# The border between the first feed-forward and the mixers of a hybrid decoder layer, written out as one order, with two mixer weights split ahead of it

## The chip, the cores and the metric

The kernel runs on one core of a Trainium2 chip. The metric is the device time of one launch in microseconds (us). The kernel before took 933.62 us (median of 3 runs, 933.32 to 933.72). One more execution was taken with the hardware profiler: it took 932.9 us, of which its instructions span 930.8 us, so 2.1 us lie around the span. All times of day below (such as "at 338.34") are us from the start of that span.

## What is computed

One decoder layer on 512 tokens of width 1024, in float32:

```python
x = x + 0.5 * rms_norm(swiglu_ffn(rms_norm(x, norm_pre[l, 0]), ffn1_w_in[l], ffn1_w_out[l]), norm_post[l, 0])
mixed = token_mixer(rms_norm(x, norm_pre[l, 1]), w_mix_in[l], ..., w_mix_out[l])
x = x + rms_norm(mixed, norm_post[l, 1])
x = x + 0.5 * rms_norm(swiglu_ffn(rms_norm(x, norm_pre[l, 2]), ffn2_w_in[l], ffn2_w_out[l]), norm_post[l, 2])
```

`swiglu_ffn` has an inner width of 2816. `token_mixer` multiplies the normed tokens by one wide matrix `w_mix_in`, runs two recurrences (HGRN2 and mLSTM) on the columns in chunks, gates and norms them, and multiplies by `w_mix_out`. The first 512 columns that the kernel takes from `w_mix_in` are the forget gates of HGRN2: a sigmoid, then `log`, then a running sum.

## The kernel before: how the work is laid out

**Tiles.** The 512 tokens lie in four tiles of 128 (tile 0 to 3). `xs` holds the residual x in float32. `xq` (four buffers, `xq_77` to `xq_80` in the order of instructions) holds the normed tokens transposed, split into a high and a low part; `xq0` and `xq1` hold tiles 0 and 1, `xq2` and `xq3` tiles 2 and 3.

**Products.** A float32 product is done as three TensorE products (PE): high by high, high by low, low by high. So each weight tile of 512 KB is loaded by DMA into a `raw` buffer (issued on the queue of SP), and then split: ScalarE (ACT) casts it to the high part (`cast`, L235), VectorE (DVE) subtracts to get the low part (L236). A split weight goes into one of `WBUF` = 4 slots of one large tile `w`. `split` (L189) does the next weight of a fixed list; `feed` splits while fewer than 4 slots are taken; `pull` calls `feed` and hands out the next split weight; `drop` frees a slot. Splitting a weight is also what issues a later load: the `raw` ring of the mixers' weights has three buffers, so load n+3 goes out once weight n is split.

**The end of the first feed-forward** (`ffn_out`, L699). The output is made in two halves of 512 columns. In the second half the first seven pairs of weight rows are done in one loop; the last four pairs (`LAST`) are left to the end, and then done tile by tile, so that the tiles become ready one after the other. The six matmuls of one tile with one of these pairs are called a half-pair here (`out_mm`, L721, matmuls at L130 to L132). Some pairs are done in a seven-product form whose corrections (`terms`) are added to the sums by DVE (`add`, L756). For tile 3 that is done ahead: one matmul (L796) opens another PSUM bank, `add` writes sum plus correction into it, and the last pairs go on there. For tiles 0 to 2 `add` comes after the last matmul. In the order of before, `mm(0)` does the last four pairs for tiles 0 and 1 in turn, and then come tiles 2 and 3.

**From a finished tile to the mixers** (`last`, L429, outside any written schedule: a scheduler orders the instructions of each engine). `post1` squares the second half of the tile on ACT (L377), makes the norm's factor with two tiny POOL (GpSimd) instructions (L378, L382), multiplies by the gain (DVE, L414) and adds to `xs` (two DVE instructions, L418). `pre` norms the new x for the mixers: two ACT squares of `xs`, three POOL instructions, two DVE products (L396) into `xn` (tiles 0 and 2, one buffer) or into a free part of `hf` (tiles 1 and 3). `turn` transposes it on PE (8 matmuls by the identity, L291), and `two` splits the result from PSUM: ACT copies the high part (L297), DVE the low part (L298).

**The head of the mixers.** `head4` (L472) multiplies the first four mixer weights (the forget gates, w0 to w3 below) by tiles 0 and 1 alone (`head_mm`, 24 matmuls each, L467), before tiles 2 and 3 are ready, and turns tiles 2 and 3 after the first and third of them. Then `forget_gates` (L1023) multiplies the same four weights by tiles 2 and 3 (L457), takes the sigmoids and so on; from there on, jobs of further mixer weights (`job_f`, `job_t`) are dealt out between the steps of the recurrences. All of that is ordered by the scheduler.

Of the kernel before, what the change touches and what calls it, by code (L numbers as in the profile page):

```python
# [14 lines left out]
P = 128  # L15
T = 512
D = 1024
# [6 lines left out]
PAIRS = NF // 2  # L24
HALF = T // 2
# [45 lines left out]
class Layer:  # L71
# [201 lines left out]
    def drop(self, w):  # L273
        self.alive -= 1
        self.free.append(self.slot.pop(id(w))[0])
# [109 lines left out]
    def pre(self, i, g):  # L385

        nc = self.nc
        x = self.xs[:, i, :]
        *_, r = self.rms([x[:, :512], x[:, 512:]])
        if i % 2:  # L390
            xn = self.hf[:, 16:18, :].rearrange("p a t -> p (a t)")
        else:
            xn = self.sp.tile([P, D], F32, tag="xn", bufs=1, name=self.name("xn"))
        for h in range(2):
            v = slice(512 * h, 512 * h + 512)
            scaled = nc.vector.scalar_tensor_tensor(xn[:, v], x[:, v], r, g[:, v], op0=ALU.mult, op1=ALU.mult)  # L396
        self.normed = [self.square, scaled]
        return xn
# [54 lines left out]
    def in_k(self, ps, w, k, hs):  # L453
        mm = self.nc.tensor.matmul
        for n, (a, b) in enumerate(((0, 0), (0, 1), (1, 0))):
            for m, (u0, u1) in enumerate(hs):
                mm(  # L457
                    ps[:, u0:u1], w[:, a, k, :], self.xop(k, b, u0, u1),
                    start=k + n + m == 0, stop=k == ND - 1 and n == 2, skip_group_check=True,
                )  # L460

    def head_mm(self, w):

        ps = self.ps()
        for m, (a, b) in enumerate(((0, 0), (1, 0), (0, 1))):
            for k in range(ND):
                self.nc.tensor.matmul(  # L467
                    ps[:, :HALF], w[:, a, k, :], self.xop(k, b, 0, HALF), start=m + k == 0, stop=m == 2 and k == ND - 1
                )
        self.head.append((w, ps))  # L470

    def head4(self, trans):  # L472

        self.head = []
        for n in range(4):
            self.head_mm(self.pull())
            if n in (0, 2):
                trans(2 + n // 2)

    def open_ffn(self, ctx):  # L480
# [4 lines left out]
        sq = [hp.tile([P, 2 * D + PAD], F32R, tag="s", bufs=3, name=self.name("sq")) for _ in range(3)]  # L485
        self.sq = [self.place(t, KH, True) for t in sq]
# [212 lines left out]
    def ffn_out(self, gpost_row, scale, after, trans, head):  # L699
# [60 lines left out]
        with self.tc.manual_schedule():  # L760
            for half in range(2):
# [6 lines left out]
                for m, k2, kind in todo:  # L768
# [5 lines left out]
                    if kind in "pr":  # L774
                        for i in range(NT):
                            out_mm(acc[i], w, h, i, m == 0, m == PAIRS - 1 or (half == 1 and i == NT - 1 and m == todo[-1][0]))
# [17 lines left out]
                else:  # L794
                    left, acc[-1] = acc[-1], sums[1]
                    self.nc.tensor.matmul(acc[-1], h[:, 0, 0, :P], w[:, 0, 0, :], start=True, stop=False, skip_group_check=True)  # L796
                    add(acc[-1], left, terms[-1])
# [5 lines left out]
            self.flush()  # L803

        def mm(i):
            for m, (k2, w) in enumerate(ws if i != 1 else ()):
                for j in (0, 1) if i == 0 else (i,):
                    out_mm(acc[j], w, hs[m][0], j, False, m == LAST - 1)
                    if m == LAST - 1 and j < NT - 1:
                        add(acc[j], acc[j], terms[j])  # L810
                if i == NT - 1:
                    self.drop(w)
                yield LAST - 1 - m

        self.last(mm, ys, acc, g, after, trans, head)
# [51 lines left out]
    def mix_items(self):  # L867
# [3 lines left out]
        def item(src, a, b, rows=None):  # L871
            key = ("mix", len(made))
            made.append(Item(key, [Load(key, src, a, b)], rows))

        def f(c0):
            for n in range(4):
                item(w[:, c0 + n * P : c0 + (n + 1) * P].rearrange("(k p) f -> p k f", p=P), ND, P)
# [707 lines left out]
def layer(tc, aps):  # L1585
    with ExitStack() as ctx:
# [26 lines left out]
        with ExitStack() as f1:  # L1613
# [18 lines left out]
            L.ffn_out(post[0:1, :], 0.5, lambda i: norm(i, 1), trans, L.head4)  # L1632
        L.mixer()
        with ExitStack() as f2:
# [3 lines left out]
            L.ffn_out(post[2:3, :], 0.5, store, lambda i: None, lambda trans: None)  # L1638
# [30 lines left out]
```

## Time and profile before

| what | before |
|---|---|
| median of 3 runs | 933.62 us |
| the profiled execution | 932.9 us |
| its span | 930.8 us |
| busy: PE, DVE, ACT, POOL | 99%, 82%, 52%, 31% |
| granted TensorE clock | 0.998 |
| first L796 of the first feed-forward to the first L457 of the forget gates | 322.09 to 362.63, 40.54 us |

The time of the whole program is the time of PE plus what PE waits, so the place to read is the list of PE's waits, and then the order of time around each of them. A row of the timeline has the start, the duration, the engine, the line, the operation with output<-input, and how many equal instructions were merged into it; brackets hold the idle time before it and what ended that. Two durations are easily mixed up: a matmul of 128x512 shows 0.39 us, since it is pipelined, but the next one starts 0.23 us later.

### The profile page before, as it was taken

The numbers are of one execution on the slowest core, as the hardware profiler recorded it, in microseconds if no ns is written. First come the engines' busy times: TensorE is split into PE (matmuls) and PEld (weight loads), VectorE is DVE, ScalarE is ACT, GpSimd is POOL, SyncE is SP. The second block draws the span as 40 slices with busy tenths as digits, with TensorE's granted clock in tenths as the row PEclk, the third lists the DMA queues.
The fourth block names the chain that finished last, engine by engine and source line by source line (L and its number), as shares of the span: only waits on it lengthen the run. The fifth ranks groups of instructions, "written<-read, shape, count | busy, mean of one in ns | idle before, by whom it ended". The sixth has DMA issues, their size and how long they took to land.

```text
span 930.8 us, 17376 instructions
## 1 busy us (share of the span) xinstructions
PE 919.6 (99%) x7239; PEld 854.7 (92%) x7239; DVE 761.0 (82%) x899; ACT 480.5 (52%) x653; POOL 290.1 (31%) x225
## 2 busy tenths in 40 slices
PE   9999999999999999999999999999999999999997
PEld 7999999999888879998888888999999999988885
DVE  6898999999868766788766665887999999986874
ACT  7644445445544544987753254853535444544541
POOL 3535555662000028000021301354555565100001
PEclk9999999999999999999999999999999999999999
DMA  9243324331323304432423136204324332233302
GB/s 320 89 137 114 114 92 136 120 109 68 112 92 99 105 1 119 112 90 70 137 69 114 46 91 203 91 27 133 114 91 136 115 114 92 68 113 97 108 23 91
DMA packets 81994, 97.14 MB, mean 104 GB/s; under 512 B 4178, under 2 KB 61558, under 8 KB 81915
## 3 DMA queue, kind: packets, MB, share of 16 engines
q1 hardware_dynamic: 81306, 94.44, 32.5%
q8 instruction: 57, 0.93, 0.4%
q0 software_dynamic: 320, 1.06, 0.4%
q10 hardware_dynamic: 288, 0.52, 0.2%
q14 instruction: 23, 0.18, 0.1%
HBM read 93.90 MB, written 2.11 MB: 103 GB/s over the span
## 4 chain that ended last, share of the span: by engine, by line
PE 61%; DVE 1%; POOL 0%; ACT 0%; issue 0%; DVEq 0%; POOLq 0%; ACTq 0%
PE ps L512 23%; PE ps L130 8%; PE ps L132 8%; PE ps L131 8%; PE ps L457 6%; PE ps L738 3%; PE ps L1168 1%; PE ps L467 1%; PE ps L291 1%; PE ps L1438 0%; PE ps L1406 0%; PE ps L1241 0%; PE ps L1207 0%; PE ps L1408 0%; PE ps L1362 0%; PE ps L1431 0%
## 5 line engine op out<-in xcount | busy, mean ns | idle before, releaser
L236 DVE TENSOR_TENSOR w<-raw,w 128x1024 fp32r<-128x1024 f32 x226 | 375.3, 1670 | 59.2 <-ACT w L235 59.0
L235 ACT CAST w<-raw 128x1024 fp32r<-128x1024 f32 x226 | 235.6, 1051 | 268.3 <-POOL raw L223 94.0
L223 POOL TENSOR_TENSOR raw<-raw,raw 128x1024 f32<-128x1024 f32 x80 | 221.0, 2764 | 175.0 <-DVE w L236 164.5
L512 PE MATMUL ps<-xq,w 128*128 128x256 f32 x2016 | 238.1, 277 | 0.0
L512 PEld LDWEIGHTS ps<-xq,w 128*128 128x128 f32 x2016 | 233.7, 188 | 0.2
L512 PE MATMUL ps<-sq,w 128*128 128x256 f32 x1440 | 171.0, 277 | 0.0
L512 PEld LDWEIGHTS ps<-sq,w 128*128 128x128 f32 x1440 | 167.4, 188 | 0.0
L131 PE MATMUL ps<-w,hs 128*128 128x512 f32 x240 | 93.7, 390 | 0.0
L130 PE MATMUL ps<-w,hs 128*128 128x512 f32 x240 | 93.7, 390 | 0.0
L132 PE MATMUL ps<-w,hs 128*128 128x512 f32 x240 | 93.6, 390 | 0.0
L130 PE MATMUL ps<-w,xq 128*128 128x512 f32 x208 | 83.2, 400 | 0.1
L131 PE MATMUL ps<-w,xq 128*128 128x512 f32 x208 | 81.1, 391 | 0.0
L132 PE MATMUL ps<-w,xq 128*128 128x512 f32 x208 | 81.0, 391 | 0.0
L378 POOL TENSOR_SCALAR col<-col 128x1 f32<-128x1 f32 x24 | 9.7, 404 | 202.6 <-ACT junk L377 202.6
L457 PE MATMUL ps<-xq,w 128*128 128x256 f32 x480 | 55.8, 279 | 0.0
L457 PEld LDWEIGHTS ps<-xq,w 128*128 128x128 f32 x480 | 55.4, 188 | 0.2 <-issue 0.2
L132 PEld LDWEIGHTS ps<-w,hs 128*128 128x128 f32 x240 | 45.1, 188 | 9.4
L130 PEld LDWEIGHTS ps<-w,hs 128*128 128x128 f32 x240 | 45.1, 188 | 8.8
L131 PEld LDWEIGHTS ps<-w,hs 128*128 128x128 f32 x240 | 45.1, 188 | 8.7
L132 PEld LDWEIGHTS ps<-w,xq 128*128 128x128 f32 x208 | 39.1, 188 | 8.7 <-DVE xq L298 0.3
L130 PEld LDWEIGHTS ps<-w,xq 128*128 128x128 f32 x208 | 39.1, 188 | 8.6 <-ACT xq L297 0.7
L131 PEld LDWEIGHTS ps<-w,xq 128*128 128x128 f32 x208 | 39.2, 188 | 7.4
(246 smaller groups left out, 1097.0 us busy)
## 6 DMA issues: line engine op xcount, KB each, us to landing
raw<-in_ffn_w_in_dram SPq DMA_DIRECT2D x88, 512.0 KB, 3.8
raw<-in_ffn_w_out_dram SPq DMA_DIRECT2D x44, 512.0 KB, 3.7
raw<-in_w_mix_in_dram SPq DMA_DIRECT2D x28, 512.0 KB, 3.8
raw<-in_w_mix_out_dram SPq DMA_DIRECT2D x8, 512.0 KB, 3.7
out_dram<-xs SPq DMA_DIRECT2D x8, 256.0 KB, 2.1
xs<-in_x_dram SPq DMA_DIRECT2D x6, 256.0 KB, 6.1
gpost<-in_norm_post_dram SPq DMA_DIRECT2D x3, 512.0 KB
gpre<-in_norm_pre_dram SPq DMA_DIRECT2D x2, 512.0 KB, 4.2
```

Source lines behind the costliest of these rows:

```text
L130: mm(ps, sh, mh, start=start, stop=False, **kw)
L131: mm(ps, sh, ml, start=False, stop=False, **kw)
L132: mm(ps, sl, mh, start=False, stop=stop, **kw)
L223: nc.gpsimd.tensor_tensor(o, o, c, op=ALU.add)
L235: lambda: nc.scalar.copy(hi, src),
L236: lambda: nc.vector.tensor_tensor(lo, src, hi.bitcast(F32), op=ALU.subtract),
L291: self.nc.tensor.transpose(pt[:, c * P : (c + 1) * P], src[:, k * P : (k + 1) * P], self.ident)
L378: nc.gpsimd.tensor_scalar(m, ss, s2 / D, b, op0=ALU.mult, op1=ALU.add)
L457: mm(ps[:, u0:u1], w[:, a, k, :], self.xop(k, b, u0, u1), start=k + n + m == 0, stop=k == ND - 1 and n == 2, skip_group_check=True,)
L467: self.nc.tensor.matmul(ps[:, :HALF], w[:, a, k, :], self.xop(k, b, 0, HALF), start=m + k == 0, stop=m == 2 and k == ND - 1)
L512: self.nc.tensor.matmul(ps[:, c], wb[b][:, k, v], left[d][:, k, :], start=first and a + n + k == 0, stop=n == 2 and k == KH - 1, skip_grou ...
L738: self.nc.tensor.matmul(out, a[:, x, ka, tok(qa, t)], b[y][:, kb, col(qb)], start=p in sums and p not in begun, stop=stop and last[p, t] = ...
```

## The change

Four things change, all around the place above.

1. The half-pairs of the last four pairs are dealt otherwise. Where (tile, pair) is a half-pair, before it was (0,0) (1,0) (0,1) (1,1) (0,2) (1,2) (0,3) (1,3); now it is (0,0) (0,1) (1,0) (0,2) (0,3) (1,1) (1,2) (1,3). Tiles 2 and 3 follow as before. This holds for both feed-forwards.
2. In the first feed-forward, tile 2 is treated as tile 3 was: a second L796 matmul opens a fresh bank, and its correction is added ahead.
3. The first two mixer weights w0 and w1 (`EARLY` = 2) are split right behind the last weights of the feed-forward, and not into the four slots but into tiles of the feed-forward's own ring `raw2`, named `early`. As they take no slot, two more weights (w4, w5) are split at the end of the border by `feed`, while before they waited for slots.
4. The whole border is written out in `border` in one order, inside `manual_schedule`, so that each engine's instructions stand as the code calls them. The steps themselves (squares, POOL factors, gains, adds, transposes, splits, head products) are the same. The second feed-forward keeps `last`.

A small tile `pad` of 256 bytes per partition shifts later addresses. The core of the diff:

```diff
+EARLY = 2
...
     def drop(self, w):
-        self.alive -= 1
-        self.free.append(self.slot.pop(id(w))[0])
+        if id(w) in self.slot:
+            self.alive -= 1
+            self.free.append(self.slot.pop(id(w))[0])
...
-    def head4(self, trans):
-
-        self.head = []
-        for n in range(4):
-            self.head_mm(self.pull())
-            if n in (0, 2):
-                trans(2 + n // 2)
+    def border(self, one, steps, ys, acc, g, gain):
...
+        posts = [self.post_steps(i, *ys[i], acc[i], g) for i in range(NT)]
...
+        deal(0)
+        for _ in range(3):
+            go(posts[0])
+        squares(0)
+        deal(1)
+        go(posts[1])
+        go(posts[1])
+        scaled(0)
+        go(posts[1])
+        squares(1)
+        for m in range(4):
+            one(2, m)
+        turned(0)
+        go(posts[2])
+        go(posts[2])
+        scaled(1)
+        go(posts[2])
+        high(0)
+        for m in range(3):
+            one(3, m)
+        squares(2)
+        low(0)
+        turned(1)
+        high(1)
+        one(3, 3)
+        low(1)
+        go(posts[3])
+        scaled(2)
+        go(posts[3])
+        go(posts[3])
+        self.head_mm(self.pull(False))
+        turned(2)
+        w2, w3 = self.split(), self.split()
+        go(w2)
+        go(w3)
+        squares(3)
+        high(2)
+        for w in (w2, w3):
+            for _ in w:
+                pass
+        scaled(3)
+        low(2)
+        self.head_mm(self.pull(False))
+        self.head_mm(self.pull(False))
+        turned(3)
+        high(3)
+        low(3)
+        self.head_mm(self.pull(False))
+        self.feed()
...
+        hp.tile([P, 64], F32, name=self.name("pad"))
...
                 else:
-                    left, acc[-1] = acc[-1], sums[1]
-                    self.nc.tensor.matmul(acc[-1], h[:, 0, 0, :P], w[:, 0, 0, :], start=True, stop=False, skip_group_check=True)
-                    add(acc[-1], left, terms[-1])
+                    for j, p in ((2, 1), (3, 5)) if head else ((3, 1),):
+                        left, acc[j] = acc[j], sums[p]
+                        self.nc.tensor.matmul(acc[j], h[:, 0, 0, :P], w[:, 0, 0, :], start=True, stop=False, skip_group_check=True)
+                        add(acc[j], left, terms[j])
...
+            for _ in range(EARLY):
+                if self.items and self.items[0].dst:
+                    self.full_split()
+
+        steps = {0: [(0, 0), (0, 1), (1, 0), (0, 2), (0, 3)], 1: [(1, 1), (1, 2), (1, 3)]}
...
+        if head:
+            with self.tc.manual_schedule():
+                self.border(one, steps, ys, acc, g, after)
+            return
...
+        def early():
+            return tuple(self.hpool.tile([P, ND, P], F32R, tag="raw2", bufs=5, name=self.name("early")) for _ in range(2))
```

In `border`, `posts[i]` has three steps (the square with its POOL factor; the gain; the two adds to `xs`), `squares(i)` is the square of the new x with its POOL factor, `scaled(i)` its two DVE products, `turned(i)` the transposes, and `high` and `low` the split of the transposed tile.

What this does to the rows of an engine shows best on VectorE, from the first finished tile to the first head product. The rows of before: `ps<-ps,hf` is a correction, `ps<-ps,gpost` a gain, `xs<-` the adds to x, `xn<-xs` and `hf<-xs` the normed tile, `xq<-ps` a low part, `w<-raw` the low part of a mixer weight.

```order
L756 TENSOR_TENSOR ps_3134<-ps_3134,hf_85 128x512
L756 TENSOR_TENSOR ps_3135<-ps_3135,hf_85 128x512
L414 TENSOR_TENSOR ps_3134<-ps_3134,gpost_2629 128x512
L418 SCALAR_TENSOR_TENSOR xs<-y_3102,col_3489,xs 128x512
L418 SCALAR_TENSOR_TENSOR xs<-ps_3134,col_3489,xs 128x512
L396 SCALAR_TENSOR_TENSOR xn_3507<-xs,col_3505,gpre_3493 128x512 x2
L414 TENSOR_TENSOR ps_3135<-ps_3135,gpost_2629 128x512
L418 SCALAR_TENSOR_TENSOR xs<-y_3109,col_3516,xs 128x512
L418 SCALAR_TENSOR_TENSOR xs<-ps_3135,col_3516,xs 128x512
L756 TENSOR_TENSOR ps_3136<-ps_3136,hf_85 128x512
L298 TENSOR_TENSOR xq_77<-ps_3584,xq_77 128x4x128
L298 TENSOR_TENSOR xq_78<-ps_3591,xq_78 128x4x128
```

The same place of the change:

```order
L237 TENSOR_TENSOR early_3436<-raw_3389,early_3435 128x1024
L237 TENSOR_TENSOR early_3442<-raw_3393,early_3441 128x1024
L862 TENSOR_TENSOR ps_3135<-ps_3135,hf_85 128x512
L561 TENSOR_TENSOR ps_3135<-ps_3135,gpost_2630 128x512
L565 SCALAR_TENSOR_TENSOR xs<-y_3103,col_3488,xs 128x512
L565 SCALAR_TENSOR_TENSOR xs<-ps_3135,col_3488,xs 128x512
L862 TENSOR_TENSOR ps_3136<-ps_3136,hf_85 128x512
L561 TENSOR_TENSOR ps_3136<-ps_3136,gpost_2630 128x512
L576 SCALAR_TENSOR_TENSOR xn_3532<-xs,col_3503,gpre_3450 128x512 x2
L565 SCALAR_TENSOR_TENSOR xs<-y_3110,col_3529,xs 128x512
L565 SCALAR_TENSOR_TENSOR xs<-ps_3136,col_3529,xs 128x512
L561 TENSOR_TENSOR ps_3131<-ps_3131,gpost_2630 128x512
```

The two early low parts stand ahead of the border, tile 0's correction, gain and adds come before tile 1's correction, and tile 2's correction (`ps_3136` in the rows of before) is gone from here.

The second place is ScalarE where the border ends and the forget gates begin. Before, `f<-ps` being the four sigmoids (`ACT_TABLE_LOAD` changes the function table ahead of a sigmoid or a logarithm):

```order
L297 CAST xq_80<-ps_3772 128x4x128
L235 CAST w<-raw_3666 128x1024
L1034 ACT_TABLE_LOAD
L1034 ACTIVATE f_3830<-ps_3676 128x512
L235 CAST w<-raw_3670 128x1024
L1034 ACTIVATE f_3830<-ps_3715 128x512
L235 CAST w<-raw_3674 128x1024
L1034 ACTIVATE f_3881<-ps_3740 128x512
L1046 ACT_TABLE_LOAD
L1046 ACTIVATE f_3830<-f_3830 128x1024
L1034 ACT_TABLE_LOAD
L1034 ACTIVATE f_3881<-ps_3779 128x512
```

And now:

```order
L499 CAST xq_80<-ps_3778 128x4x128
L236 CAST w<-raw_3445 128x1024
L236 CAST w<-raw_3714 128x1024
L1158 ACT_TABLE_LOAD
L1158 ACTIVATE f_3847<-ps_3662 128x512
L1158 ACTIVATE f_3847<-ps_3723 128x512
L1170 ACT_TABLE_LOAD
L1170 ACTIVATE f_3847<-f_3847 128x1024
L1158 ACT_TABLE_LOAD
L1158 ACTIVATE f_3898<-ps_3748 128x512
L1158 ACTIVATE f_3898<-ps_3787 128x512
L236 CAST w<-raw_3717 128x1024
```

The casts of w4 and w5 stand together ahead of the first sigmoid, and those of w6 and w7 behind the fourth. On PE the order of the border and of the mixers is the same as before but for the dealing of the half-pairs, the second L796 and one place where the two halves of tile 1's transposes now stand together. On SP the small load of the gate weights (`graw`) stands two loads later than before. On POOL nothing moves.

87 lines of the change are left out of this document (67 added, 20 removed).

## The prediction

> **What bounds the kernel now.** I read the page first, then the list of PE's waits, then the stretch of the border, then each engine's order of time in it. The page's busy line:
>
> ```profile
> PE 919.6 (99%) x7239; PEld 854.7 (92%) x7239; DVE 761.0 (82%) x899; ACT 480.5 (52%) x653; POOL 290.1 (31%) x225
> ```
>
> PE is busy nearly all the time, so only PE's waits and PE's own work can move the end. All of PE's waits:
>
> ```profile
> PE ps L467 <- DVE w L236: 1.7, 2, 1.0
> PE ps L126 <- POOL ident masks.py:199: 1.6, 1, 1.6
> PE ps L291 <- DVE xn L396: 0.5, 1, 0.5
> PE ps L291 <- DVE hf L396: 0.3, 1, 0.3
> PE ps L512 <- ACT xq L311: 0.2, 1, 0.2
> ```
>
> Two of the five lie at the program's start (L126, L512). The other three, 2.5 us, lie in the border. Behind it PE waits for nothing, in the mixers and in the second feed-forward, so what the border gains reaches the end unless a new wait takes it. The border and the 40 us behind it, busy us by engine:
>
> ```profile
> 322.09:362.63 40.54, 37.92 (x226) 32.49 (x225) 28.92 (x39) 19.39 (x39) 16.69 (x35) 1.00 0.19 50
> 362.63:402.63 40.00, 40.00 (x361) 39.50 (x360) 25.98 (x40) 35.81 (x37) 9.09 (x20) 1.00 0.38 100
> ```
>
> In the border the columns PE, PEld, DVE, ACT, POOL show PE idle for 2.62 us and DVE and ACT far from full. Behind it ACT (35.81 of 40) is the engine with the least room. PE's order of time through the border, pieces:
>
> ```profile
> 322.31 0.39 PE L130 MATMUL ps<-w,hs 128*128 128x512 f32 x1
> ...
> 338.41 0.39 PE L132 MATMUL ps<-w,xq 128*128 128x512 f32 x1
> 339.25 1.29 PE L291 MATMUL ps<-ident,xn 128*128 128x128 f32 x8 [0.46 <-DVE xn L396]
> 340.30 0.47 PE L130 MATMUL ps<-w,hs 128*128 128x512 f32 x1
> ...
> 343.83 0.39 PE L130 MATMUL ps<-w,hs 128*128 128x512 f32 x1
> 344.56 0.66 PE L291 MATMUL ps<-ident,hf 128*128 128x128 f32 x4 [0.35 <-DVE hf L396]
> ...
> 347.41 1.07 PE L467 MATMUL ps<-xq,w 128*128 128x256 f32 x8
> 349.48 2.10 PE L467 MATMUL ps<-xq,w 128*128 128x256 f32 x16 [0.99 <-DVE w L236]
> ...
> 355.04 4.15 PE L467 MATMUL ps<-xq,w 128*128 128x256 f32 x34 [0.73 <-DVE w L236]
> 359.02 1.04 PE L291 MATMUL ps<-ident,hf 128*128 128x128 f32 x8
> 359.81 2.98 PE L467 MATMUL ps<-xq,w 128*128 128x256 f32 x24
> 362.63 9.57 PE L457 MATMUL ps<-xq,w 128*128 128x256 f32 x83
> ```
>
> Four waits: for tile 0's normed x, for tile 1's, and twice for the low part of a mixer weight (w0, then w1).
>
> **What PE's own work comes to.** The stretch from the first L796 (322.09) to the first L457 took 40.54. I price the new stretch without waits. From 322.31 to 338.41 lie 71 matmuls, 0.2268 each; 96 half-pair matmuls and now two L796 (one added: 0.23) make 98 x 0.2268 = 22.23. A turn of 8 that waits for nothing takes 359.81 - 359.02 = 0.79, four make 3.16. A head product of 24 takes 362.63 - 359.81 = 2.82, four make 11.28. After a turn the next 15 matmuls took 343.83 - 340.30 = 3.53, 0.13 over 15 x 0.2268; twice, 0.26. Sum 36.93, which is 3.61 less than 40.54.
>
> **Are the operands there?** I keep the clock of the trace: first L796 at 322.09, second at 322.31, half-pairs from 322.54 on, 1.36 each. The rows from which DVE, ACT and POOL are timed:
>
> ```profile
> 325.87 1.22 DVE L236 TENSOR_TENSOR xq<-hf,xq 128x1024 fp32r<-128x1024 f32 x1
> 332.03 0.70 DVE L756 TENSOR_TENSOR ps<-ps,hf 128x512 f32<-128x512 f32 x1 [4.94 <-PE ps L132]
> 334.60 0.74 DVE L418 SCALAR_TENSOR_TENSOR xs<-y,col,xs 128x512 f32<-128x512 f32 x1
> 335.25 0.75 DVE L418 SCALAR_TENSOR_TENSOR xs<-ps,col,xs 128x512 f32<-128x512 f32 x1
> 338.34 1.43 DVE L396 SCALAR_TENSOR_TENSOR xn<-xs,col,gpre 128x512 f32<-128x512 f32 x2 [2.34 <-POOL col L382]
> ```
>
> ```profile
> L235 ACT CAST w<-raw 128x1024 fp32r<-128x1024 f32 x226 | 235.6, 1051 | 268.3 <-POOL raw L223 94.0
> ```
>
> ```profile
> 332.77 0.60 ACT L377 ACTIVATE junk<-ps 128x512 f32<-128x512 f32 x1 [7.31 <-DVE ps L756]
> ```
>
> ```profile
> raw<-in_w_mix_in_dram SPq DMA_DIRECT2D x28, 512.0 KB, 3.8
> ```
>
> *Early splits.* They cost two low parts of 1.2 on DVE and two casts of 1.05 on ACT, and lie in the idle 4.94 (DVE) and 7.31 (ACT) ahead of the first correction: DVE is through with them at about 329.6. w0 and w1, the two that PE waited for, are then ready 16 us ahead. Without that cover their 2.4 would come ahead of tile 0's correction. Their raw buffers come free at 329 and not at 349, so the next loads (3.8 each) go out 20 us sooner.
>
> *Half-pairs.* Tile 0 is complete after five, at 329.5 instead of 332.0. Against that, half-pair (0,3) needs its low part at 328.4 instead of 331; DVE made it at 327.09 and makes it some 0.2 later now, since the cast behind the second L796 starts 0.2 later. Cover 1.1; (0,2), whose low part ends as that of (0,3) begins, at 325.9, needs it at 327.1 instead of 328.4, cover 1.0. The second correction made ahead (0.70) fits, as DVE waits for that cast anyway. In the second feed-forward the same cover holds and nothing is added.
>
> *Tile 0.* Correction 329.6 to 330.3; factor 1.8 behind it, as 332.73 to 334.60 shows; the two adds, 1.4 from 334.60 to 336.00, end at 333.5. From the first add's end (335.34) to the normed product (338.34) went 3.0, so POOL's factor is there at 335.8; the product of 1.43, behind tile 1's gain (336.0), ends at 337.4. PE turns tile 0 at 322.54 + 12 x 1.36 = 338.87. Cover 1.4; before, it waited.
>
> *Tile 1.* Complete at 333.6, its adds stand behind tile 0's product: 337.4 to 338.8; 3.0 after the first one's end (338.1) stands the factor, at 341.1, and the normed x ends at 342.5. PE turns it at 338.87 + 0.79 + 0.13 + 3 x 1.36 = 343.87. Cover 1.4. w0's product starts behind the last half-pair, at 343.87 + 0.79 + 0.13 + 1.36 = 346.15; the two casts of tile 1 (0.6 each, as ACT's other 128x512 above) end at 345.9.
>
> *Tile 2.* It needs no correction now. Its adds stand behind tile 1's product, 342.5 to 343.9; the factor is there at 343.2 + 3.0 = 346.2, DVE with tile 1's low parts through at 346.7, the normed x at 348.1; turned at 346.15 + 2.82 = 348.97. Cover 0.9.
>
> *w2 and w3.* Cast behind tile 3's square, 347.1 to 349.2; low parts behind tile 3's gain and adds (348.1 to 350.1), so 350.1 to 352.4. w1's product starts at 348.97 + 0.79 = 349.76 and w2's at 352.58; w2's low part, there at 351.3, is first used by the ninth matmul, at 353.5. Cover 2.2.
>
> *Tile 3.* Here POOL and DVE meet, so this is priced from the row where they met before:
>
> ```profile
> 354.09 2.07 POOL L378 TENSOR_SCALAR col<-col 128x1 f32<-128x1 f32 x1 [2.43 <-ACT junk L377]
> ```
>
> ```profile
> L378 POOL TENSOR_SCALAR col<-col x24: 190/190/2072, 5.1 to 870.8; 128x1 f32<-128x1 f32 x24
> ```
>
> ```profile
> 353.77 2.35 DVE L236 TENSOR_TENSOR w<-raw,w 128x1024 fp32r<-128x1024 f32 x2
> 357.19 1.41 DVE L396 SCALAR_TENSOR_TENSOR hf<-xs,col,gpre 128x512 f32<-128x512 f32 x2 [1.08 <-POOL col L382]
> ```
>
> A POOL instruction on 128x1 took 2.07, until DVE's two low parts were over (356.12). In the change the low parts of w2 and w3 again run just as POOL should make tile 3's factor. Held to 352.4, the factor comes 1.1 later, as 356.12 to 357.19 shows, and the normed x is made from 353.5 to 354.9. PE turns tile 3 at 352.58 + 2.82 = 355.40. Cover 0.5. The Trainium skill has the rule in its page "GPSIMD Engine Reference", section "8. Key points": GpSimd shares its SBUF interfaces with VectorE and contends with instructions that have two SBUF inputs. The trace agrees (2.07 where the median of the same instruction is 0.19, and the two overlap a low part to within 0.04 at their ends), and without it the factor would be there at 352.2 and the cover 1.8; the sum is the same by both, and what hangs on the rule is the first rival below.
>
> The first L457 then stands at 355.40 + 0.79 + 2.82 = 359.01. Every cover is positive, so the sum is PE's own work: 3.61 gained. I take **3.5**, 0.1 for a cover that is off. The covers are estimates from these rows. The least (0.3 at w0's product, 0.5 at tile 3, 0.9 at tile 2) stand in one chain, so being off by half a microsecond costs some 0.2, by a whole one 0.7.
>
> **What could take it back behind the border.** PE reaches the mixers 3.5 earlier; their other engines must too.
>
> ```profile
> 363.42 0.76 POOL L1227 MEMSET gw<- 128x800 int32 x1
> ```
>
> ```profile
> 403.78 0.61 ACT L1153 ACTIVATE ke<-el 128x512 f32<-128x512 f32 x1
> ```
>
> ```profile
> 411.11 1.09 PE L1168 MATMUL ps<-qe,ke 128*32 128x64 f32 x34
> ```
>
> A wait is added: the memory of the early tiles is reused, so POOL's MEMSET of `gw` and SP's `graw` load now wait until w1 is used for the last time, at 359.0 + 2 x 2.82 = 364.6. Queued behind on POOL are the masks. POOL works 9.09 in the 40 us behind the border, so all of that is over by 364.6 + 9.1 = 374 (without the wait it would be about 1.2 sooner). Their first reader is the DVE instruction that makes `el`, which ACT reads at 403.78: cover some 25, cost nothing. Behind `graw` on SP stands the load of a weight whose raw buffer comes free only at some 373: nothing. `graw` itself is moved past two raw loads, which wait for splits that end before 360.
>
> On ACT the table loads are as many as before; two casts are already done when the sigmoids begin, and the first sigmoid's source is there 3.5 sooner. `ke` ends at 404.39 for a PE that comes at 411.11: cover 6.7, and 3.2 even if ACT did not move at all. So nothing is subtracted.
>
> **Sum.** The profiled execution: 932.9 - 3.5 = 929.4 (the span 930.8 becomes 927.3, the 2.1 around it stay). The median of the runs lies 0.72 above that execution, so 933.62 - 3.5 = **930.1**. A measurement of this kernel tells 0.2%, 1.9 us, from no change.
>
> **Rivals.**
>
> *POOL held longer.* The low parts of w2 and w3 hold POOL at more than its first instruction, by another 1.9 (2.07 - 0.19): beyond the cover of 0.5 PE waits 1.4 at tile 3's turn. (The page named above stands behind this one.) For it: the hold is in the trace. Against: nothing else with two SBUF inputs stands on DVE then but the product that waits for POOL. Gain 2.1, 931.5.
>
> *The mixers give part back.* ACT's queue comes there later than before, and not sooner: the cover of 3.2 decides; 5 us later makes PE wait 1.8. For it: ACT is at 35.81 of 40 and its order there is dealt anew. Against: the same count of instructions, two fewer casts in the way. Gain 1.7, 931.9.
>
> *It doesn't do what it says.* A transposed tile or weight is again late, another wait in the place of each removed one, 2.5 or so: 932.6 to 933.6. For it: three covers are below 1. Against: the four waits would all have to come back.
>
> *Slower.* ACT's queue now holds the casts of w4 and w5 ahead of all four sigmoids. w5's load goes out when w2's low part is done (351.3) and lands 3.8 later, at 355.1; its cast is due at 358, behind tile 3's two and w4's. If that load is late, sigmoids, logarithms and `ke` are late with it. Cover 2.9 at the cast and 6.7 at L1168; slower by 0.2% only from 2.9 + 6.7 + 3.5 + 1.9 = 15 us of lateness on. 18 us would give 930.1 + 18 - 9.6 = 938.5. Against: no load in this trace takes long, and DMA's share in the border is 0.19.
>
> **How the numbers follow.** Forecast (gain 3.1 to 3.7) 0.66; POOL 0.12; mixers 0.10; doesn't do it 0.05; slower 0.07. The forecast's own times are 929.9 to 930.5; with the scatter of the runs (0.3 below the median) and the overdrawn covers the range begins at 929.4, and it takes in POOL (931.5) and the mixers' case (931.9) with the same scatter up to 932.3. Faster by over 0.2% (below 931.75): forecast, most of POOL and a little of the mixers, 0.78. Within: 0.15. Slower: 0.07.
>
> **What would show it.** Right: no wait of PE at L291 or at the head products; 36.9 to 37.1 from the first L796 to the first product of the second round; early low parts over by 330; POOL's factor for tile 3 held to the end of w3's low part, and yet no wait at the third turn. Wrong: a wait at the third turn (POOL), at (0,3), or at L1168 or a job in the mixers (ACT).

## The result, and the profile after

The change takes 929.47 us (median of 6 runs, 928.58 to 930.53) where the kernel before, run beside it, takes 933.66 (933.32 to 933.79): 4.2 us less, a ratio of 0.9954 (95% interval 0.9942 to 0.9965). The prediction was 930.1, with 929.9 to 930.5 as the forecast's own times and a range from 929.4 to 932.3. So the gain came, and it is larger than was forecast. The profiled execution of the change is the slowest of its six, 930.53 with a span of 928.8.

The busy line of the page and the list of PE's waits, complete:

```profile
PE 919.5 (99%) x7240; PEld 855.8 (92%) x7240; DVE 761.7 (82%) x899; ACT 480.8 (52%) x653; POOL 285.6 (31%) x225
```

```profile
PE ps L127 <- POOL ident masks.py:199: 1.6, 1, 1.6
PE ps L293 <- DVE xn L395: 0.9, 1, 0.9
PE ps L618 <- ACT xq L313: 0.2, 1, 0.2
```

The busy line hardly differs, and the list is the answer: no wait of the border is left in it. All three lie at the program's start, and the one that is new there (0.9 at L293, the turn of the first normed tile) is no effect of the border: the profile of the same kernel taken once more (further down) doesn't have it. ScalarE's first square, which waits for the load of x, starts at 5.56, where in the profile of before it started at 4.31:

```profile
5.56 0.63 ACT L379 ACTIVATE junk<-xs 128x512 f32<-128x512 f32 x1 [2.37 <-DMA xs<-in_x_dram]
```

So this execution began late. From its hundredth matmul to the border all of PE lies 1.89 behind the execution of before, and 1.89 is to be subtracted wherever a time of day below is held against one of the prediction.

The border: its engines (PE, PEld, DVE, ACT, POOL), and PE's order of time in it, half-pairs left out (L903 opens the banks, L293 turns, L466 are head products, L456 the second round):

```profile
323.98:360.88 36.90, 36.90 (x227) 32.94 (x226) 30.11 (x40) 21.14 (x41) 14.69 (x37) 1.00 0.22 58
```

```profile
323.98 0.62 PE L903 MATMUL ps<-w,hs 128*128 128x512 f32 x2
...
340.76 1.04 PE L293 MATMUL ps<-ident,xn 128*128 128x128 f32 x8
...
345.74 1.04 PE L293 MATMUL ps<-ident,hf 128*128 128x128 f32 x8
...
348.00 2.90 PE L466 MATMUL ps<-xq,early 128*128 128x256 f32 x24
350.74 1.03 PE L293 MATMUL ps<-ident,xn 128*128 128x128 f32 x8
351.53 3.07 PE L466 MATMUL ps<-xq,early 128*128 128x256 f32 x24
354.44 2.99 PE L466 MATMUL ps<-xq,w 128*128 128x256 f32 x24
357.27 1.04 PE L293 MATMUL ps<-ident,hf 128*128 128x128 f32 x8
358.06 2.98 PE L466 MATMUL ps<-xq,w 128*128 128x256 f32 x24
360.88 0.39 PE L456 MATMUL ps<-xq,early 128*128 128x256 f32 x2
```

PE is busy in all of the 36.90, no bracket stands behind any row, and the start of each row is the end of the one before it in PE's own pitch. Before, the same stretch took 40.54. Now the rows of VectorE that PE would have waited for, the two early low parts and the four normed tiles:

```profile
329.12 2.35 DVE L237 TENSOR_TENSOR early<-raw,early 128x1024 fp32r<-128x1024 f32 x2
...
337.75 1.41 DVE L576 SCALAR_TENSOR_TENSOR xn<-xs,col,gpre 128x512 f32<-128x512 f32 x2
...
342.85 1.40 DVE L576 SCALAR_TENSOR_TENSOR hf<-xs,col,gpre 128x512 f32<-128x512 f32 x2
...
348.25 1.40 DVE L576 SCALAR_TENSOR_TENSOR xn<-xs,col,gpre 128x512 f32<-128x512 f32 x2
...
354.94 1.41 DVE L576 SCALAR_TENSOR_TENSOR hf<-xs,col,gpre 128x512 f32<-128x512 f32 x2 [0.80 <-POOL col L384]
```

The time from the end of such an operand to the moment when PE needs it is called its cover, as in the prediction. Each normed tile ends 1.60, 1.49, 1.09 and 0.92 ahead of its turn (340.76 - 339.16, 345.74 - 344.25, 350.74 - 349.65, 357.27 - 356.35). The prediction had 1.4, 1.4, 0.9 and 0.5. Its smallest cover, 0.3 at w0's product, came out at 0.50: ScalarE's copies of tile 1 end at 347.50 and the product starts at 348.00.

```profile
346.45 1.05 ACT L499 CAST xq<-ps 128x512 fp32r<-128x512 f32 x2
```

POOL's factor for tile 3:

```profile
352.12 0.94 POOL L380 TENSOR_SCALAR col<-col 128x1 f32<-128x1 f32 x1 [1.70 <-ACT junk L379]
353.15 1.12 POOL L380 TENSOR_SCALAR col<-col,col 128x1 f32<-128x1 f32 x1
354.35 0.55 POOL L384 TENSOR_TENSOR col<-col,nhalf 128x1 f32<-128x1 f32 x1
```

It is held as predicted, until the low parts of w2 and w3 are over at 354.14 (they run from 351.79, 2.35 long), though by two instructions (0.94, 1.12) and not by one of 2.07, and still PE doesn't wait. In the mixers the pair that the prediction named:

```profile
401.94 0.63 ACT L1277 ACTIVATE ke<-el 128x512 f32<-128x512 f32 x1
```

```profile
409.36 0.35 PE L1292 MATMUL ps<-qe,ke 128*32 128x64 f32 x5
```

`ke` ends at 402.57 and PE comes at 409.36: 6.8 to spare, as before.

**Where the 4.2 us are.** The profiles of all kernels below split alike into four terms: the start, 302.67 to 302.93 from the hundredth matmul to the border, the border, and 567.8 to 568.2 behind it. The border gives 40.54 - 36.90 = 3.64. Behind it 568.17 (930.80 - 362.63) became 567.94 (928.82 - 360.88), 0.23 less. And the runs' times exceed their spans by 1.7 in every run of the change, by 2.0 to 2.1 in those of before: 0.31 between the medians (2.04 and 1.73). The sum is 4.18. The spans vary from run to run by more than a microsecond in both kernels, in the profiles through the start, and the sum leaves the start out; that it meets the difference of the medians this closely is partly luck.

### The profile page after: what moved, and what is told of

Read it like the earlier page. It is cut to its first block, busy times and chain, and to the rows that moved or that the text cites. A ratio compares the mean times of both kernels' runs of the same rounds, so it can differ in the third digit from the quotient of the medians.

```text
span 928.8 us, 17377 instructions
## 1 busy us (share of the span) xinstructions
PE 919.5 (99%) x7240; PEld 855.8 (92%) x7240; DVE 761.7 (82%) x899; ACT 480.8 (52%) x653; POOL 285.6 (31%) x225
## 4 chain that ended last, share of the span: by engine, by line
PE 98%; issue 1%; DMA 0%; ACT 0%; DVE 0%; POOL 0%; DVEq 0%; POOLq 0%; SPq 0%; ACTq 0%
PE ps L618 46%; PE ps L131 11%; PE ps L133 11%; PE ps L132 11%; PE ps L844 6%; PE ps L456 6%; PE ps L293 1%; PE ps L466 1%; PE ps L1292 1%; DMA xs<-in_x_dram 0%; PE ps L1562 0%; PE ps L1530 0%; PE ps L1365 0%; PE ps L1331 0%; PE ps L1532 0%
## 5 line engine op out<-in xcount | busy, mean ns | idle before, releaser
L237 DVE TENSOR_TENSOR w<-raw,w 128x1024 fp32r<-128x1024 f32 x224 | 370.6, 1665 | 56.0 <-ACT w L236 55.7
L618 PE MATMUL ps<-xq,w 128*128 128x256 f32 x2016 | 238.1, 277 | 0.0
L618 PEld LDWEIGHTS ps<-xq,w 128*128 128x128 f32 x2016 | 233.7, 188 | 0.2
L380 POOL TENSOR_SCALAR col<-col 128x1 f32<-128x1 f32 x24 | 7.8, 324 | 203.4 <-ACT junk L379 203.3
L456 PE MATMUL ps<-xq,w 128*128 128x256 f32 x432 | 50.4, 278 | 0.0
L456 PEld LDWEIGHTS ps<-xq,w 128*128 128x128 f32 x432 | 49.9, 188 | 0.2 <-issue 0.2
```

The source lines that it names most:

```text
L237: lambda: nc.vector.tensor_tensor(lo, src, hi.bitcast(F32), op=ALU.subtract),
L456: mm(ps[:, u0:u1], self.both(w)[a][:, k, :], self.xop(k, b, u0, u1), start=k + n + m == 0, stop=k == ND - 1 and n == 2, skip_group_check=True,
L618: self.nc.tensor.matmul(ps[:, c], wb[b][:, k, v], left[d][:, k, :], start=first and a + n + k == 0, stop=n == 2 and k == KH - 1, skip_grou ...
```

## The experiments

The border's length is read from each profile, from the first opening matmul to the first product of the second round; these two rows are quoted where the verdict rests on them.

### The early weights alone

```diff
+            for _ in range(EARLY):
+                if self.items and self.items[0].dst:
+                    self.full_split()
```

This edit, with the raw buffers for w0 and w1, was made in the kernel before. The kernels of this and the next two experiments have `pad` in them as well; by itself it moves nothing, as a run further down shows.

> The kernel before with only the two early weights (w0 and w1 split behind the last feed-forward weights into raw buffers); half-pairs, banks and the scheduler's order as before. Theory (each removed wait counts for itself): PE's waits at the head products are gone, those at the turns of tiles 0 and 1 stay. In the trace of before the wait for w0's low part made the step 347.41 to 349.48 1.13 longer than 8 matmuls of 0.1175, that for w1's 352.45 to 355.04 0.71 longer than 16, and the turn between them 0.24 longer than 0.79: border (first opening matmul to first product of the second round) 40.54 - 2.1 = 38.4, time 933.6 - 2.1 = 931.5. Rival (a wait only moves): PE comes to the turns of tiles 2 and 3 some 1 to 2 earlier and waits there: border 39.5 to 40.5, time 932.6 to 933.6.

Measured: 932.44 us, ratio 0.9988 (0.9979 to 0.9997). PE's rows at the ends of the border and at its first and longest wait:

```profile
322.96 0.39 PE L799 MATMUL ps<-w,hs 128*128 128x512 f32 x1
```

```profile
339.86 1.29 PE L293 MATMUL ps<-ident,xn 128*128 128x128 f32 x8 [0.19 <-DVE xn L398]
...
351.93 1.38 PE L293 MATMUL ps<-ident,xn 128*128 128x128 f32 x8 [0.92 <-DVE xn L398]
...
362.58 0.28 PE L459 MATMUL ps<-xq,early 128*128 128x256 f32 x1
```

Border 39.62, so 0.92 gained and not 2.1. The rival holds: the waits at the head products are gone, and PE, coming earlier, waits 0.92 at tile 2's turn, where the list of before has no wait. The border lies in the rival's range, the time 0.2 below it.

### The dealing alone

```diff
+        steps = {0: [(0, 0), (0, 1), (1, 0), (0, 2), (0, 3)], 1: [(1, 1), (1, 2), (1, 3)]}
...
+                    for j, p in ((2, 1), (3, 5)) if head else ((3, 1),):
```

Again in the kernel before, with its splits and its scheduler.

> The kernel before with only the new dealing of the half-pairs and the fresh bank for tile 2; w0 and w1 are split into slots as before, and the scheduler orders the border. Theory: the turns of tiles 0 and 1 no longer wait (in before they cost 0.87 and 0.62 over their unwaited pitch), the second opening matmul costs 0.23, and the waits for w0 and w1 stay as long as they were, since their casts follow the slots that PE frees: border 40.54 - 1.5 + 0.23 = 39.3, time 932.4. Rival 1: what the turns gain is waited for at w0 and w1: border 40.5 to 40.8, time 933.6 to 933.9. Rival 2: the dealing alone makes the weights come sooner too: border 37 to 38.

Measured: 933.94 us, ratio 1.0001 (0.9992 to 1.0010); border 364.78 - 323.20 = 41.58, 1.0 longer than before in this profile. No theory came out as it was written. Rival 1 is nearest, as what the turns gain is waited for at w0's product, though not for the weight. (The 1.0 has to do with the clock of this execution: see the next experiment.) The turns wait for nothing now, but at w0's product two other waits stand:

```profile
347.94 2.12 PE L467 MATMUL ps<-xq,w 128*128 128x256 f32 x16 [0.56 <-ACT xq L297]
352.05 1.68 PE L467 MATMUL ps<-xq,w 128*128 128x256 f32 x8 [1.98 <-DVE xq L298]
```

The scheduler has put the low parts of w0 and w1 and tile 2's normed product ahead of tile 1's low parts, for which PE, now early, must wait 1.98. From this came a new theory: on VectorE the order decides, not the dealing or the early splits as such. The next run is its test.

### Early weights and dealing, without the written order

The two edits above together, `last` and `head4` as before.

> The kernel before with the early weights, the new dealing and the fresh bank, but the border ordered by the scheduler: after without the written order. Theory (the written order is what turns the two parts into time): on VectorE the low parts of w2 and w3 stand ahead of tile 2's normed product and of tile 1's low parts, as those of w0 and w1 did in the kernel with the dealing alone, and w0's product waits for tile 1's low part by the same 2.0 and for its high part by 0.6: border 41.0 to 41.6, time 933.0 to 934.3. Rival (the two parts add up: 0.9 from the early weights, and the dealing no longer collides with w0 and w1, as they are split): border 37 to 38, time 929.5 to 930.5.

Measured: 932.90 us, ratio 0.9995 (0.9986 to 1.0004), which isn't told from no gain. PE's rows, and then PE's clock behind the wait (the column behind POOL's):

```profile
322.95 0.62 PE L800 MATMUL ps<-w,hs 128*128 128x512 f32 x2
```

```profile
347.42 2.14 PE L469 MATMUL ps<-xq,early 128*128 128x256 f32 x16 [0.28 <-ACT xq L299]
351.43 1.34 PE L469 MATMUL ps<-xq,early 128*128 128x256 f32 x8 [1.88 <-DVE xq L300]
352.61 1.76 PE L293 MATMUL ps<-ident,xn 128*128 128x128 f32 x8
354.03 3.99 PE L469 MATMUL ps<-xq,early 128*128 128x256 f32 x24
357.85 2.89 PE L469 MATMUL ps<-xq,w 128*128 128x256 f32 x24
...
364.18 0.39 PE L459 MATMUL ps<-xq,early 128*128 128x256 f32 x2
```

```profile
352.00:354.00 2.00, 2.00 (x14) 1.97 (x13) 2.00 (x4) 1.31 (x4) 0.00 (x0) 0.69 0.34 85
354.00:356.00 2.00, 2.00 (x11) 2.00 (x10) 2.00 (x2) 1.62 (x5) 1.62 (x2) 0.50 0.01 4
356.00:358.00 2.00, 2.00 (x19) 2.00 (x18) 1.20 (x3) 0.00 (x0) 1.92 (x5) 0.96 0.79 212
```

Border 364.18 - 322.95 = 41.23, in the theory's range (the time is 0.1 below it), and by the theory's mechanism: w0's product waits 1.88 for tile 1's low part (2.0 was expected) and 0.28 for its high part (0.6 was expected). But part of the length is the clock, for which the theory had no term. Behind the wait it is 0.50 for 3.4 us: 2.00 x 0.31 / 0.50 = 1.24 in the first of the three rows, 2.00 in the second and 0.16 in the third. There w1's product takes 357.85 - 354.03 = 3.82 where the same product takes 2.82 elsewhere, and the turn ahead of it 1.42 and not 0.79, together 1.6 us that no bracket shows. Not all of that is the clock's, as a turn behind a wait is longer at full clock too. From the end of the long wait to the second round it is 12.75 here (364.18 - 351.43) and 11.68 for the same work in the kernel of the next experiment, whose clock stays at 1.00 (362.15 - 350.47). So the clock is worth about 1.1, and without its fall the border would be some 40.2, an estimate, hardly shorter than before.

The times agree: the median is 0.8 below that of before, run beside it (933.71), and 0.3 of that lies around the span. So the two parts together, left to the scheduler, bring next to nothing, and that 41.23 lies in the theory's range is in part luck. The dealing alone is a like case. From the end of its long wait to the second round it takes 12.73 (364.78 - 352.05), so the 1.0 by which its border exceeds that of before is about what the clock took.

### One block of the written order moved

```diff
         high(1)
+        w2, w3 = self.split(), self.split()
+        for w in (w2, w3):
+            for _ in w:
+                pass
         one(3, 3)
         low(1)
```

The same lines are gone from behind `turned(2)`. All else as in the change.

> The kernel after with one block of the written order moved: casts and low parts of w2 and w3 stand behind tile 1's copies and so ahead of tile 1's low parts on VectorE, where the scheduler put them in the kernel without the written order (border 41.23). All else as after. Theory (this one place is what the written order is worth): w2's low part follows its cast at some 348.5 on after's clock, tile 1's low parts come at 350.7 to 352.0 instead of 347.0 to 348.3, w0's product waits 1.4 to 2.0 for them, and tile 2's turn some 0.2 to 0.5: border 38.6 to 39.6; where the granted clock falls to 0.50 behind that wait, as it did in the two kernels with a wait of 1.9, another 1.0 to 1.6, so that the spans of the runs fall into two groups, 929.0 to 930.5 and 930.5 to 932. Rival (the order's worth lies elsewhere): border 36.9 to 37.5, one group of spans, 927 to 928.5.

Measured: 931.85 us, ratio 0.9983 (0.9974 to 0.9992); border 362.15 - 322.96 = 39.19.

```profile
346.98 2.00 PE L466 MATMUL ps<-xq,early 128*128 128x256 f32 x16
350.47 1.34 PE L466 MATMUL ps<-xq,early 128*128 128x256 f32 x8 [1.50 <-DVE xq L503]
```

The theory holds in its size: this one block, 2.35 us of VectorE that stand ahead of tile 1's low parts and not behind them, costs 39.19 - 36.90 = 2.29. (The two casts move with it on ScalarE, but the wait is for VectorE.) It is not all that the written order is worth. The border without the written order is longer by another 2.04: 1.07 behind the wait, where the clock fell there and stayed at 1.00 in this profile (12.75 against 11.68), and 0.97 up to the end of the wait, which is longer there (1.88) and has the 0.28 ahead of it. The two groups of spans come out about as expected: eight of the eleven runs span 929.4 to 930.5, three 931.3 to 932.3, and two of those three have the lowest mean clock, 0.996.

### The early splits moved late

In the change the two `full_split` were moved from ahead of the border to behind `low(1)`.

> The kernel after with the two early splits moved from ahead of the border to behind tile 1's low parts, about where the kernel before had them; all else, the written order too, as after. Theory (the place of the two low parts is what pays): w0's cast then follows tile 1's copies, w0's product waits some 0.7, tile 2's normed x stands 2.4 later on VectorE and its turn waits some 0.8 more: border 38.2 to 39.0 where after has 36.90, time 930.8 to 931.6. Rival (VectorE has room anyway, the order and the dealing carry the gain): border 36.9 to 37.2, time 929.4 to 929.8.

Measured: 931.13 us, ratio 0.9973 (0.9963 to 0.9982); border 361.01 - 322.49 = 38.52, in the range of the theory.

```profile
347.30 3.36 PE L466 MATMUL ps<-xq,early 128*128 128x256 f32 x24 [0.62 <-ACT early L236]
350.50 1.19 PE L293 MATMUL ps<-ident,xn 128*128 128x128 f32 x8
```

The place of the early splits is worth 1.6. Only 0.62 of it stands in a bracket, and the wait of 0.8 that the theory had at tile 2's turn isn't there as one. The rest is in the rows and the pauses between them. Against the change, w0's product starts 0.79 later behind tile 1's turn (347.30 - 344.25 = 3.05, and 348.00 - 345.74 = 2.26), lasts 0.46 longer (350.50 - 347.30 = 3.20, and 350.74 - 348.00 = 2.74), and the turns of tiles 2 and 3 last 0.15 and 0.22 longer. A short wait inside a merged row has no bracket of its own.

### The dealing of before, with all else of the change

```diff
+        if head:
+            steps = {0: [(0, 0), (1, 0), (0, 1), (1, 1), (0, 2), (1, 2), (0, 3), (1, 3)], 1: []}
```

> The kernel after with the half-pairs of the first feed-forward's border dealt as before (tiles 0 and 1 in turn); early weights, fresh bank and written order stay. Theory (the dealing pays at the turns of tiles 0 and 1): tile 0 is complete 2.7 later than in after, its correction and gain stand behind tile 1's correction, its normed x is 2.5 to 3.5 later where after had 2.3 to spare for the first half, and its turn waits 0.3 to 0.9, tile 1's up to 0.5 more: border 37.3 to 38.3, time 0.4 to 1.4 above after. Rival (with the written order the dealing is idle): border 36.9 to 37.0, time as after.

Measured: 930.96 us, ratio 0.9973 (0.9963 to 0.9983); border 360.98 - 322.26 = 38.72, so the dealing is worth 1.8 within the change. The theory's direction is right and its size was too small: tile 0's turn waits 0.47, and a second wait stands where it expected none, at w0's product, for ScalarE's copy of tile 1:

```profile
339.67 1.29 PE L293 MATMUL ps<-ident,xn 128*128 128x128 f32 x8 [0.47 <-DVE xn L576]
...
348.09 3.12 PE L466 MATMUL ps<-xq,early 128*128 128x256 f32 x24 [0.64 <-ACT xq L499]
```

### Two more low parts ahead of tile 3

```diff
+        for n, (w, _) in zip((2, 3), list(self.ready)[-2:]):
+            hi, lo = self.both(w)
+            nc.vector.tensor_tensor(lo, self.raw["mix", n], hi.bitcast(F32), op=ALU.subtract)
```

> The kernel after with the low parts of w2 and w3 computed twice, so that VectorE does 2.35 more ahead of tile 3's normed product. In after that product started at 354.94 and PE turned tile 3 at 357.27. Theory A (POOL gets its next tiny instruction in whenever one low part ends, as at 353.06 and 354.27 in after): the factor is there before the last low part ends, the product starts 1.6 later than in after (356.5), its first half is there at 357.2 and the second at 357.9, PE waits 0.2 to 0.4: border 37.1 to 37.4, time 0.2 to 0.5 above after. Theory B (POOL is held through the whole run of low parts, as the 2.07 in before looked like; the rival of the prediction): the factor is there 0.8 behind the last of them, product from 357.3, PE waits 1.0 to 1.4: border 37.9 to 38.4, time 1.0 to 1.5 above after.

Measured: 930.11 us, ratio 0.9964 (0.9952 to 0.9977); border 360.57 - 322.95 = 37.62, between the two theories. VectorE's low parts run from 350.74 to 355.37. POOL's factor, and PE's turn of tile 3:

```profile
351.07 0.94 POOL L380 TENSOR_SCALAR col<-col 128x1 f32<-128x1 f32 x1 [1.69 <-ACT junk L379]
352.10 2.18 POOL L380 TENSOR_SCALAR col<-col,col 128x1 f32<-128x1 f32 x1
354.36 1.41 POOL L384 TENSOR_TENSOR col<-col,nhalf 128x1 f32<-128x1 f32 x1
```

```profile
356.70 1.29 PE L293 MATMUL ps<-ident,hf 128*128 128x128 f32 x8 [0.32 <-DVE hf L579]
```

POOL finishes an instruction about where a low part ends, after one (0.94) or after two (2.18), and the factor is there 0.40 behind the last of them. Two low parts more, 2.35, put tile 3's normed product only 1.90 later after the opening matmul than in the change (355.81 - 322.95 against 354.94 - 323.98). The rival of the prediction, POOL held by another 1.9 beyond the low parts, does not come about: twice the low parts cost 0.72. The bracket shows 0.32 of that; a turn that waits lasts 1.05 (357.75 - 356.70) and not 0.79, and the pause ahead of it is in neither.

### Without the second bank, and without pad

```diff
-                    for j, p in ((2, 1), (3, 5)) if head else ((3, 1),):
+                    for j, p in ((3, 1),):
```

> The kernel after without the fresh bank for tile 2: no second opening matmul, tile 2's correction behind its last half-pair as before. Theory (the bank buys nothing, as tile 2 has cover): PE's own work is one matmul less, 0.23, and the correction delays tile 2's gain by only 0.2, since ScalarE is busy with tile 1's squares until then: border 36.90 - 0.23 = 36.67, no wait at the turns of tiles 1 and 2, time 0.2 below after. Rival (the bank is needed): the correction's 0.70 on VectorE makes tile 1's or tile 2's turn wait, border 37.0 to 37.5, time 0.1 to 0.6 above after.

Measured: 929.22 us, ratio 0.9953 (0.9941 to 0.9966); border 359.80 - 323.12 = 36.68, no wait of PE in it. The theory holds to 0.01 in the border: tile 2's fresh bank buys nothing here and costs its one matmul. The times can't tell 0.2 us.

> The kernel after without the tile pad. Theory (pad does the 0.3): border 36.9, time minus span 2.0, time 0.3 above after, 929.8. Rival: border 36.9, time minus span 1.7, time 929.5. If pad kept PE or VectorE from something inside the program, the border or the 568.0 behind it would be longer than in after.

Measured: 928.98 us, ratio 0.9954 (0.9939 to 0.9969); border 36.91, time minus span 1.71.

> The kernel before with the small tile pad and nothing else. Question: after's times exceed its spans by 1.7, those of before by 2.0 to 2.1, and this 0.3 has no term in the prediction. Theory (pad's shift of addresses does it): border 40.5 as before, time minus span 1.7, time 933.3. Rival (it comes with the new program, not with pad): border 40.5, time minus span 2.0, time 933.6.

Measured: 933.57 us, ratio 1.0001 (0.9992 to 1.0010); border 40.54, time minus span 2.03. The theory fell in both: pad moves nothing, here or there. The 0.3 around the span appears in every kernel whose instructions stand in another order, the early weights alone and the dealing alone included, and its cause stays open. The stores to `out`, which come up below, don't explain it: with the early weights alone they begin as late as before (930.74 - 915.18 = 15.6 ahead of the span's end), and yet that kernel's times exceed its spans by 1.7.

> The kernel after without the fresh bank for tile 2 and without pad: what the runs so far point to as the shortest. Theory: border 36.68, no wait of PE in it, 567.9 behind it, 0.2 below after: 928.8 to 929.4. Rival: tile 2's correction is now overdrawn without pad's addresses, border over 36.9, no gain.

Measured: 929.23 us, ratio 0.9948 (0.9935 to 0.9960); border 36.68. It has the shortest border of all, but by times it can't be told from the change.

### The change once more

> The kernel after once more, unchanged, for the split of its time into start, border and rest, and to stand beside the next kernel on one chip. Theory (start, 302.8, border and 568 are four separate terms, and only the start varies from run to run): border 36.9, first opening matmul 302.8 behind the hundredth matmul, 567.9 from the second round to the end, the spans of its runs 926.9 to 928.8 apart by the start alone; time 929.0 to 929.6. Rival (the border itself varies): border off by over 0.1 from 36.9.

Measured: 929.12 us, ratio 0.9946 (0.9932 to 0.9959); border 36.91, 302.82 ahead of it from the hundredth matmul, 568.00 behind it, spans 926.9 to 928.0. The border repeats to 0.01, and the runs differ by their start.

## What the prediction had right, and the step that failed

- **PE's own work.** The sum 36.93 stands against 36.90 measured, the border's gain 3.61 against 3.64. It held since it priced the stretch without waits. Adding up the brackets of before (0.46 + 0.35 + 0.99 + 0.73 = 2.53, less 0.23 for the added matmul) would have given 2.3: a wait costs more than its bracket.
- **The covers.** All were positive, as the prediction had them. The early low parts are over at 331.47 - 1.89 = 329.6, as worked out. The least three, at w0's product (0.3), tile 3 (0.5) and tile 2 (0.9), came out at 0.50, 0.92 and 1.09. The 0.1 taken off "for a cover that is off" was not used up.
- **Half-pairs and early weights.** The dealing is worth 1.8 and the place of the early splits 1.6 within the change, and both together, left to the scheduler, nothing that the times tell from before. The prediction read its covers from VectorE's new order, so it contained this, but did not say that the order is what they hang on: the block of w2 and w3 alone costs 2.3 when it stands ahead of tile 1's low parts. No run has the written order without the other two parts, so what it is worth alone isn't shown.
- **POOL held longer.** The hold came as said, and the rival did not: the factor is there 0.4 to 0.8 after the last low part, with two of them and with four.
- **The mixers** gave nothing back: 6.8 to spare at `ke`, against 6.7 worked out. The slower rival, w5's load, left no trace: no wait of PE behind the border.
- **The step that failed** is a term of the sum: "the span 930.8 becomes 927.3, the 2.1 around it stay". The sum took what lies around the span as fixed and gave no reason for it. The time around the span did not stay; it is 1.7, which is 0.31 of the 4.2, and why stays open. And "in the second feed-forward the same cover holds and nothing is added" left out what is behind the border: 0.23 less, most of it behind the last matmul. From the start of the last matmul to the end of the span, the three profiled kernels with the old dealing in the second feed-forward take 7.07 to 7.08, all others 6.72 to 6.92. With the new dealing the stores to `out` begin earlier, 18.1 ahead of the span's end and not 15.6, as the rows of SP's queue show, first of before and then of the change. That may be why, but no run here tests it.

```profile
915.25 12.48 SPq L1611 DMA_DIRECT2D out_dram<-xs  x8
```

```profile
910.70 15.23 SPq L1735 DMA_DIRECT2D out_dram<-xs  x8
```

Forecast 3.5, measured 4.2: the 0.7 between them are 0.1 of caution, 0.31 around the span, 0.23 behind the border, and 0.03 in the border. So 929.47 lies below the forecast's own times, and at the edge of the range: the 929.4 at which it begins was 929.9 less an allowance, 0.3 of it for the scatter of the runs. The ratio of 0.9954, applied to the 933.62 from which the prediction set out, gives 929.3, and the same kernel once more took 929.12; both lie below the range. The mechanism was right, and what the sum held fixed was mis-sized by 0.54.

## What to carry to other kernels

Price a stretch of a saturated engine by its own work without waits and then check the covers, and not by adding up the brackets: two waits that look separate share one VectorE, and taking one away moves the other. Read covers from the order in which the helping engine's instructions will stand; the same parts that gain 3.6 us of the border in one order gain, in another, next to nothing. A run's time is start, middle and what lies around the span, and a few tenths of a microsecond are decided in the parts that the change isn't about.

## What the runs showed of the hardware

- A wait of 1.9 us can cost TensorE half its clock for 3.4 us. It did so in both profiles with a wait of that length (1.98 and 1.88), where the clock is 0.50 from 352.8 to 356.2, about a microsecond after the wait is over. It did not in those with 0.99 or 1.50. In the runs of the three kernels with waits of 1.5 and more the mean granted clock is 0.996 or 0.997 in 7 of 11, 3 of 10 and 2 of 11 runs, and 0.998 or 0.999 in the others; of 75 runs of the kernel before, beside them, 3 have 0.997 and none has 0.996. With the dealing alone the four runs at 0.998 and 0.999 span 930.4 to 930.9, the seven at 0.996 and 0.997 span 932.0 to 933.8. Without the written order the two groups are less clean: one of its runs at 0.998 spans 933.0.
- Where the wait falls seems to matter too. In the clock records of all fourteen traces the clock changes only at whole multiples of 3.413 us behind its first rise (341.33 is 100 of them, 914.77 is 268). Laid out in such steps, the waits of 1.98 and 1.88 each lie whole in one step (349.43 to 352.84, and 349.35 to 352.76), and the clock falls when that step ends and is back one step later. The wait of 1.50 lies across a border, 1.08 in one step and 0.42 in the next. That a step with too much idle time costs the clock of the next is read from these profiles, and no run tests it.
- The Trainium skill, "TensorE: Matmul & The Clock Gate", section "HAM oscillation — how this bites in real kernels", gives as the rule no idle gaps of TensorE above about 3.4 us; the trace disagrees, since gaps of 1.88 and 1.98 were enough here. That the same program shows the fall in one run and not in the next agrees with what the Trainium skill says in Part 1 of that page, by which the window that is watched runs free of the program.
- POOL's tiny instructions, beside a row of low parts on VectorE, end about where one of these ends, after one or after two (0.94, 1.12, 2.18 where 0.19 and 0.27 are usual).
- A bracket of 0.32 at a turn stood for 0.72 of lost time.
